# Weight sums of gate and up, and one operand sum, moved from VectorE to GpSimd in a two-FFN decoder layer

## The chip, the cores and the metric

The kernel runs on one core of a Trainium2 chip, in one launch. The metric is the device time of that core in microseconds (us), the median of several executions. PE is TensorE, DVE is VectorE, ACT is ScalarE, POOL is GpSimd and SP is SyncE, whose queue issues nearly all transfers.

## The reference: what is computed

One inference step of a hybrid decoder layer for 1,048 tokens (16 meta tokens, 1,024 prompt tokens, 8 samples), model width 1,024, in float32:

```python
h = h + 0.5 * swiglu(rmsnorm(h, n1), w1g, w1u, w1d)          # first FFN, d_ff = 2816
u = rmsnorm(h, nm) @ w_in                                     # HGRN2 heads and Mamba-2 heads
h = h + concat(hgrn_out, ssm_out) @ w_out
h = h + 0.5 * swiglu(rmsnorm(h, n2), w2g, w2u, w2d)           # second FFN
# swiglu(x, wg, wu, wd) = (silu(x @ wg) * (x @ wu)) @ wd
```

The change touches only the gate and up products `x @ wg` and `x @ wu` of the two FFNs.

## The kernel before

A float32 operand is split into a high part, rounded to the matmul's input format, and a low part, the difference; a product is three matmuls (L163 high by high, L164 high by low, L165 low by high). ACT makes each high part (`hi`, L462 for weights; `cast`, L346 for operands), DVE each low part (`lo`, L466; `low`, L352).

The gate and up products of one block of 128 hidden columns (`pair`) use a Strassen-like scheme: seven block products in place of eight, on sums of weight tiles and sums of operand blocks. `Left` holds the weights of a pair: four loaded tiles of 128x512 in buffers `r` (of which there are eight) and four sums made of them, for products 5, 6, 7 and 3, by `Left.sum_` (L458). A sum is read by `hi` and `lo`, which write the split weight into a buffer `ws`. `Left.plan` says before which product each load, sum, `hi` and `lo` stands. `Blocks` holds the moving operands: `Blocks.sum_` (L341) makes the sums for products 5, 6, 7 and 4, once per half of the tokens and per FFN, on tiles of 128x1048 (first FFN) or 128x1032 (second).

Each FFN has 22 pairs, two to a step `i` of the loop in `ffn`. From `i` = 3 on, the two pairs of a step share part of their work in an inner scheme (`Inner`), with its own small sums and splits on DVE (L586 to L601) and its own evictions (L639 to L646). The text calls these *inner pairs*: eight steps, so eight first and eight second pairs in each FFN. The other six pairs of an FFN are *plain*.

A product accumulates in PSUM. The outer products take turns in two pairs of banks, named `acc`; the inner ones use four single banks, named `mis`. A bank is free for another product when the results have been read out: by ACT (L674), or by DVE at L669, L676, L683, L685, L689, L698 and L703 (`post`), each of which reads one `acc` tile. L643 and L646 read `mis`.

Inside `ffn` the orders of PE, DVE, ACT and SP are written out by hand (`manual_schedule`): each of these engines works through its own list and waits at the head of it. POOL is not in that list, and a scheduler places its instructions. Before the change POOL's work is: constants and masks at the start (L1077 to L1112), the sums of squares for the norms (L230, `tensor_add` on two SBUF tiles), and some memsets.

`first1` and `first2` write out the order at the start of each FFN, where operands are made while the first products run.

Of the kernel before, what the change touches and what calls it, by code (L numbers as in the profile page):

```python
# [316 lines left out]
class Blocks:  # L317
# [19 lines left out]
    def sum_(self, p):  # L337
        x, y = {5: (7, 1), 6: (3, 5), 7: (3, 7), 4: (2, 6)}[p]
        x, y = self.b[x], self.b[y]
        t = self.b[p] if p == 7 else self.new(p)  # L340
        self.K.nc.vector.tensor_sub(t, x, y)  # L341

    def cast(self, p):
        hi = self.K.slot("u", self.K.T, F32R)
# [96 lines left out]
class Left:  # L441
# [12 lines left out]
    def sum_(self, p):  # L454
        x, y, op = {5: (7, 4, ALU.add), 6: (5, 1, ALU.subtract), 7: (1, 7, ALU.subtract), 3: (2, 6, ALU.subtract)}[p]
        if p not in self.raw:
            self.raw[p] = self.K.raw(self.n * P)
        self.K.nc.vector.tensor_tensor(self.raw[p], self.raw[x], self.raw[y], op)  # L458

    def hi(self, p):  # L460
        self.w[p] = self.K.ws()
# [393 lines left out]
def down(K, S, wdv, hidden, src, h, after):  # L855
# [24 lines left out]
    def pieces(p, j, g, b, tag, late=0):  # L880
# [33 lines left out]
        if p in (5, 6, 7, 3):  # L914
            x, y = {5: (21, 22), 6: (0, 11), 7: (22, 0), 3: (12, 0)}[p]
            S.before(b - 9, lambda: sum_(x, y, ALU.add if p == 5 else ALU.subtract))
# [1350 lines left out]
```

## Time and profile before

| | |
|---|---|
| median of 3 runs | 1979.23 us (1977.53 to 1981.9) |
| the profiled execution | 1973.32 us, of which the span is 1971.5 us |
| mean granted TensorE clock | 0.994 |
| PE busy | 1923.6 us (98%) |
| DVE busy | 1529.7 us (78%), 2720 instructions |
| ACT busy | 859.9 us (44%) |
| POOL busy | 82.7 us (4%), 135 instructions |
| gate and up of the first FFN | to about 460 us |
| gate and up of the second FFN | about 1280 to 1700 us |

A row of the timeline has start, duration, engine, line, operation, output<-input tiles, shapes and count, and in brackets the idle time of the engine before it and what ended it. A row of windows has, for a stretch of the span, its length, then the busy time of each engine with its number of instructions, the granted clock, the DMA share and GB/s. The durations of neighbouring DVE rows overlap by some 0.07 us, so the spacing of starts is the time that one takes in a packed queue.

### The profile page before, as it was taken

The numbers are of one execution on the slowest core, as the hardware profiler recorded it, in microseconds if no ns is written. First come the engines' busy times: TensorE is split into PE (matmuls) and PEld (weight loads), VectorE is DVE, ScalarE is ACT, GpSimd is POOL, SyncE is SP. The second block draws the span as 40 slices with busy tenths as digits, with TensorE's granted clock in tenths as the row PEclk, the third lists the DMA queues.
The fourth block names the chain that finished last, engine by engine and source line by source line (L and its number), as shares of the span: only waits on it lengthen the run. The fifth ranks groups of instructions, "written<-read, shape, count | busy, mean of one in ns | idle before, by whom it ended". The sixth has DMA issues, their size and how long they took to land.

```text
span 1971.5 us, 40943 instructions
## 1 busy us (share of the span) xinstructions
PE 1923.6 (98%) x16585; PEld 1885.4 (96%) x16585; DVE 1529.7 (78%) x2720; ACT 859.9 (44%) x1647; POOL 82.7 (4%) x135
## 2 busy tenths in 40 slices
PE   7999999999999999999999999999999999999997
PEld 6999999999999999998988989999999999999997
DVE  7788888888788776675755557888888888878973
ACT  7533232324534555465644535752332333354352
POOL 4000000000001310000000001200000000000000
PEclk9999999999999999999999999999999999999999
DMA  7233333335976632222522153224332333587851
GB/s 220 77 98 97 98 107 96 108 93 171 302 240 214 184 117 61 69 88 73 167 82 72 61 169 126 85 82 119 92 108 87 103 103 112 160 251 230 275 178 68
DMA packets 323877, 258.45 MB, mean 131 GB/s; under 512 B 17568, under 2 KB 299424, under 8 KB 323680
## 3 DMA queue, kind: packets, MB, share of 16 engines
q1 hardware_dynamic: 323448, 255.79, 42.1%
q8 instruction: 131, 2.15, 0.4%
q14 instruction: 58, 0.48, 0.1%
q0 software_dynamic: 224, 0.04, 0.0%
q10 hardware_dynamic: 16, 0.00, 0.0%
HBM read 190.79 MB, written 65.05 MB: 130 GB/s over the span
## 4 chain that ended last, share of the span: by engine, by line
PE 87%; DVE 7%; ACT 2%; DMA 2%; issue 1%; POOL 0%; SPq 0%; DVEq 0%; ACTq 0%; POOLq 0%
PE acc L163 26%; PE acc L165 26%; PE acc L164 26%; PE mis L163 1%; PE mis L165 1%; PE mis L164 1%; DVE u L352 1%; DMA s<-in_x_prompt_dram 1%; PE mis L1725 1%; PE mis L1449 0%; PE mis L1782 0%; DVE ws L466 0%; PE mis L1445 0%; DVE u L341 0%; DVE t L301 0%
## 5 line engine op out<-in xcount | busy, mean ns | idle before, releaser
L163 PE MATMUL acc<-u,ws 128*128 128x258 f32 (+3 forms) x4248 | 1242.9, 293 | 6.7 <-ACT t L674 1.7
L164 PE MATMUL acc<-u,ws 128*128 128x258 f32 (+3 forms) x4248 | 1232.1, 290 | 2.9 <-DVE u L352 2.7
L165 PE MATMUL acc<-u,ws 128*128 128x258 f32 (+3 forms) x4248 | 1231.1, 290 | 3.5 <-DVE ws L466 3.4
L163 PEld LDWEIGHTS acc<-u,ws 128*128 128x128 f32 x4248 | 803.9, 189 | 12.2 <-ACT t L674 2.1
L164 PEld LDWEIGHTS acc<-u,ws 128*128 128x128 f32 x4248 | 806.5, 190 | 5.8 <-DVE u L352 4.0
L165 PEld LDWEIGHTS acc<-u,ws 128*128 128x128 f32 x4248 | 803.6, 189 | 5.2 <-DVE ws L466 4.8
L466 DVE TENSOR_TENSOR ws<-r,ws 128x512 fp32r<-128x512 f32 x276 | 190.6, 691 | 75.0 <-ACT ws L462 74.9
L462 ACT CAST ws<-r 128x512 fp32r<-128x512 f32 x276 | 160.1, 614 | 13.3 <-ACT ws L462 7.8
L458 DVE TENSOR_TENSOR r<-r,r 128x512 f32<-128x512 f32 x176 | 121.5, 692 | 2.7 <-DMA r<-in_w_ffn_up_dram 1.2
L681 ACT ACTIVATE t<-t 128x516 f32<-128x516 f32 (+1 forms) x41 | 26.2, 639 | 212.9 <-DVE t L669 212.9
L712 ACT ACTIVATE t<-t 128x524 f32<-128x524 f32 (+1 forms) x47 | 29.9, 639 | 196.1 <-DVE t L669 196.1
L846 DVE TENSOR_TENSOR u<-u,u 128x1048 fp32r<-128x1048 f32 (+3 forms) x84 | 97.0, 1156 | 5.3 <-ACT u L842 4.5
L669 DVE TENSOR_TENSOR t<-t,u 128x524 f32<-128x524 f32 (+1 forms) x135 | 92.9, 697 | 2.8
L230 POOL TENSOR_TENSOR t<-t,t 128x262 f32<-128x262 f32 (+1 forms) x56 | 54.4, 981 | 823.6 <-ACT t L229 820.4
L158 DVE TENSOR_TENSOR ws<-r,ws 128x512 fp32r<-128x512 f32 x88 | 60.5, 698 | 36.0 <-ACT ws L157 35.6
L903 ACT CAST ws<-u 128x512 fp32r<-128x512 f32 (+1 forms) x72 | 42.2, 586 | 103.2 <-DVE u L898 100.2
L932 DVE SCALAR_TENSOR_TENSOR s<-acc,s 128x524 f32<-128x524 f32 (+3 forms) x88 | 54.6, 643 | 36.9 <-PE acc L165 36.5
L842 ACT CAST u<-u 128x1048 fp32r<-128x1048 f32 (+3 forms) x84 | 82.8, 988 | 0.0
L908 DVE TENSOR_TENSOR ws<-r,ws 128x512 fp32r<-128x512 f32 (+1 forms) x84 | 57.6, 693 | 22.3 <-ACT ws L903 22.2
L903 ACT CAST ws<-r 128x512 fp32r<-128x512 f32 (+1 forms) x84 | 47.9, 582 | 61.6 <-DVE r L898 37.0
L157 ACT CAST ws<-r 128x512 fp32r<-128x512 f32 x88 | 53.7, 618 | 35.6 <-PE acc L165 30.6
L908 DVE TENSOR_TENSOR ws<-u,ws 128x512 fp32r<-128x512 f32 (+1 forms) x72 | 47.4, 658 | 26.8 <-ACT ws L903 26.8
(417 smaller groups left out, 2297.9 us busy)
## 6 DMA issues: line engine op xcount, KB each, us to landing
r<-in_w_ffn_down_dram SPq DMA_DIRECT2D x128, 256.0 KB
hd<-s SPq DMA_DIRECT2D x93, 258.0 KB
r<-in_w_ffn_gate_dram SPq DMA_DIRECT2D x88, 256.0 KB
r<-in_w_ffn_up_dram SPq DMA_DIRECT2D x88, 256.0 KB
hd<-s SPq DMA_DIRECT2D x77, 262.0 KB
u<-hd SPq DMA_DIRECT2D x36, 516.0 KB
u<-hd SPq DMA_DIRECT2D x28, 524.0 KB
r<-in_w_in_dram SPq DMA_DIRECT2D x56, 256.0 KB
```

The lines of the kernel that those rows point to most:

```text
L158: self.nc.vector.tensor_sub(lo, src, hi.bitcast(F32))
L163: mm(ps, whi, xhi, start=first, stop=False, skip_group_check=more)
L164: mm(ps, whi, xlo, start=False, stop=False, skip_group_check=more)
L165: mm(ps, wlo, xhi, start=False, stop=last, skip_group_check=more)
L458: self.K.nc.vector.tensor_tensor(self.raw[p], self.raw[x], self.raw[y], op)
L462: self.K.nc.scalar.copy(self.w[p][:, : self.n * P], self.raw[p])
L466: self.K.nc.vector.tensor_sub(t[:, 512 : 512 + w], self.raw[p], t[:, :w].bitcast(F32))
L669: nc.vector.tensor_mul(t, t if src is None else src, spread.lanes(i, cs))
L842: K.nc.scalar.copy(hi, lo.bitcast(F32))
L846: K.nc.vector.tensor_sub(lo, lo.bitcast(F32), hi.bitcast(F32))
L903: nc.scalar.copy(w[p, j, g][:, : n * P], src)
L908: nc.vector.tensor_sub(t[:, 512 : 512 + n * P], box[0], t[:, : n * P].bitcast(F32))
```

## The change

All 176 weight sums, and 4 of the 16 operand sums (product 7, once for each half of the tokens and each FFN), are issued on POOL in place of DVE.

```diff
@@ class Blocks
         t = self.b[p] if p == 7 else self.new(p)
-        self.K.nc.vector.tensor_sub(t, x, y)
+        eng = self.K.nc.gpsimd if p == 7 else self.K.nc.vector
+        eng.tensor_sub(t, x, y)
@@ class Left
         if p not in self.raw:
             self.raw[p] = self.K.raw(self.n * P)
-        self.K.nc.vector.tensor_tensor(self.raw[p], self.raw[x], self.raw[y], op)
+        self.K.nc.gpsimd.tensor_tensor(self.raw[p], self.raw[x], self.raw[y], op)
```

The changed file has one line more ahead of these places, so its lines are numbered one higher (L458 becomes L459). The orders of PE and SP are the same as before; those of ACT and DVE are the same but for the moved instructions and a few neighbours changing places ahead of the second FFN.

On DVE, in the second pair of an inner step of the first FFN, this stood before (tiles `r` are weights and their sums, `ws` split weights, `acc` products, `s` hidden blocks):

```order
L676 TENSOR_TENSOR t_512_3946<-acc_511_3919,t_509_3912 128x524
L818 TENSOR_TENSOR s_513_3948<-s_474_3633 128x524
L718 TENSOR_TENSOR s_501_3848<-t_488_3741,t_494_3778 128x524
L466 TENSOR_TENSOR ws_514_3950<-r_480_3687,ws_514_3950 128x512
L458 TENSOR_TENSOR r_515_3966<-r_505_3880,r_507_3896 128x512
L458 TENSOR_TENSOR r_516_3968<-r_515_3966,r_504_3878 128x512
L669 TENSOR_TENSOR t_517_3982<-acc_506_3882,u_148_851 128x524
L818 TENSOR_TENSOR s_513_3948<-s_501_3848,s_513_3948 128x524
L458 TENSOR_TENSOR r_505_3880<-r_504_3878,r_505_3880 128x512
L466 TENSOR_TENSOR ws_518_3988<-r_504_3878,ws_518_3988 128x512
```

The same place on DVE has now:

```order
L677 TENSOR_TENSOR t_512_3946<-acc_511_3919,t_509_3912 128x524
L819 TENSOR_TENSOR s_513_3948<-s_474_3633 128x524
L719 TENSOR_TENSOR s_501_3848<-t_488_3741,t_494_3778 128x524
L467 TENSOR_TENSOR ws_514_3950<-r_480_3687,ws_514_3950 128x512
L670 TENSOR_TENSOR t_517_3982<-acc_506_3882,u_148_851 128x524
L819 TENSOR_TENSOR s_513_3948<-s_501_3848,s_513_3948 128x524
L467 TENSOR_TENSOR ws_518_3988<-r_504_3878,ws_518_3988 128x512
```

The sums are gone from between the low part `ws_514` and the read of bank `acc_506`. On POOL the sums of these two inner pairs stand one after the other, with nothing between that would tie them to the place in DVE's list:

```order
L459 TENSOR_TENSOR r_491_3760<-r_480_3687,r_483_3705 128x512
L459 TENSOR_TENSOR r_480_3687<-r_479_3685,r_480_3687 128x512
L459 TENSOR_TENSOR r_492_3762<-r_491_3760,r_479_3685 128x512
L459 TENSOR_TENSOR r_497_3801<-r_484_3707,r_492_3762 128x512
L459 TENSOR_TENSOR r_515_3966<-r_505_3880,r_507_3896 128x512
L459 TENSOR_TENSOR r_505_3880<-r_504_3878,r_505_3880 128x512
L459 TENSOR_TENSOR r_516_3968<-r_515_3966,r_504_3878 128x512
L459 TENSOR_TENSOR r_523_4024<-r_508_3898,r_516_3968 128x512
```

At the start of the first FFN, POOL's list runs from the last masks through the sums of the first pair, the first operand sum, the sums of the second pair and the second operand sum (`u` are operand blocks):

```order
L1082 CAST mask16_8832<-mf_1140_8829 32x16 x4
L459 TENSOR_TENSOR r_53_301<-r_18_147,r_19_149 128x512
L459 TENSOR_TENSOR r_65_346<-r_53_301,r_14_139 128x512
L459 TENSOR_TENSOR r_18_147<-r_14_139,r_18_147 128x512
L459 TENSOR_TENSOR r_71_379<-r_17_145,r_65_346 128x512
L342 TENSOR_TENSOR u_37_223<-u_39_228,u_37_223 128x1048
L459 TENSOR_TENSOR r_121_622<-r_75_394,r_86_444 128x512
L459 TENSOR_TENSOR r_75_394<-r_74_392,r_75_394 128x512
L459 TENSOR_TENSOR r_122_624<-r_121_622,r_74_392 128x512
L459 TENSOR_TENSOR r_126_660<-r_87_446,r_122_624 128x512
L342 TENSOR_TENSOR u_60_323<-u_84_439,u_60_323 128x1048
```

So the first weight sum stands behind the constants, and the second operand sum behind all sums of the second pair.

## The prediction

> **What bounds the kernel now.** I read the page first, then the windows, then the timeline of POOL and DVE side by side.
>
> ```profile
> PE 1923.6 (98%) x16585; PEld 1885.4 (96%) x16585; DVE 1529.7 (78%) x2720; ACT 859.9 (44%) x1647; POOL 82.7 (4%) x135
> L908 DVE TENSOR_TENSOR ws<-r,ws 128x512 fp32r<-128x512 f32 (+1 forms) x84 | 57.6, 693 | 22.3 <-ACT ws L903 22.2
> ```
>
> ```profile
> 35.00:75.00 40.00, 35.00 (x254) 32.90 (x252) 30.23 (x45) 30.73 (x62) 0.00 (x0) 0.96 0.17 54
> 120.00:460.00 340.00, 340.00 (x2791) 339.92 (x2790) 294.32 (x499) 103.46 (x193) 0.00 (x0) 1.00 0.33 101
> 1330.00:1700.00 370.00, 370.00 (x3083) 369.48 (x3082) 319.43 (x542) 113.11 (x211) 0.00 (x0) 1.00 0.34 102
> ```
>
> Through nearly all of gate and up PE is busy in 340.00 of 340 and 370.00 of 370 us: nothing can be gained there by a lighter DVE. Only the starts have idle PE: 5.0 us in 35 to 75, more before it. DVE is not the bound, but at 294 of 340 us it has little room, and it empties PE's banks. POOL has no work at all in these windows, so no row shows POOL beside DVE there. Other places do.
>
> **What a POOL sum costs, and whom.**
>
> ```profile
> L230 POOL TENSOR_TENSOR t<-t,t x56: 730/756/3406, 627.0 to 1287.2; 128x262 f32<-128x262 f32 x28, 128x258 f32<-128x258 f32 x28
> ```
> ```profile
> L1112 POOL TENSOR_TENSOR sel<-sel,s 16x8 f32<-16x8 f32 x1 | 0.2, 193 | 0.0
> ```
> ```profile
> 671.69 2.34 POOL L230 TENSOR_TENSOR t<-t,t 128x262 f32<-128x262 f32 x2 [4.36 <-ACT t L229]
> 1220.81 0.74 POOL L230 TENSOR_TENSOR t<-t,t 128x258 f32<-128x258 f32 x1 [0.26 <-ACT t L229]
> ```
> ```profile
> 671.01 1.24 DVE L846 TENSOR_TENSOR u<-u,u 128x1048 fp32r<-128x1048 f32 x1
> 672.17 2.27 DVE L908 TENSOR_TENSOR ws<-r,ws 128x512 fp32r<-128x512 f32 x2
> 1221.01 0.42 DVE L1850 TENSOR_TENSOR s<-s,acc 128x258 f32<-128x258 f32 x1 [0.80 <-PE acc L165]
> ```
>
> POOL's add takes 0.756 us (median) for 262 columns and 0.193 us for 8: (0.756 - 0.193) / 254 = 2.2 ns a column. My estimate from these is 0.193 + 504 x 2.2 ns = 1.31 us for a weight sum and 2.50 us for 1048 columns. The nearest rows bound a weight sum: not under 0.756, and 0.756 x 512 / 262 = 1.48 if there is no fixed part.
>
> The more important reading is in the pairs of rows. While two POOL adds run from 671.69 to 674.03, the two L908 on DVE take 2.27 us in place of about 1.3 (0.69 each, overlapped), and the adds take 2.34 in place of 1.5. They exclude each other and take turns. L1850, which has one input in PSUM, runs at 1221.01 inside a POOL add and takes its 0.42 us. So a DVE instruction with two SBUF inputs waits out a POOL add whole, and one that reads PSUM goes through, unless it is queued behind one that waits.
>
> The Trainium skill, *SBUF — State Buffer*, section "SBUF: two separate sides", says the same as a rule: GpSimd shares a port pair with VectorE instructions that have two SBUF inputs, as an exclusive lock held for the full instruction; the trace agrees in the 2.27 us above. The skill's *GPSIMD Engine Reference*, section 3.1, gives 4497 ns for a two-input add of 2,048 columns; a quarter of that, an estimate of 1.12 us, would in the layout below leave a stall of 1.2 us in a second inner pair and none in a first, and with smaller starts about 2010 us.
>
> **The change part by part.** *Removed:* 176 sums from DVE. Two in a row take 331.63 to 332.96 (below), 0.65 each: 2.6 us a pair, plus four operand sums of 1.16 us spacing. PE never waits for these in the steady windows, so they buy nothing there by themselves.
>
> *Added:* four POOL sums a pair, 5.2 us in which DVE's two-input work stands still; net 2.6 us of delay in a pair of 20 us. What decides is where they fall. POOL is not tied to DVE's list: a sum starts when its buffers are ready, and the four come in a burst that takes turns with DVE. In the **second inner pair**:
>
> ```profile
> 328.58 0.69 DVE L466 TENSOR_TENSOR ws<-r,ws 128x512 fp32r<-128x512 f32 x1 [0.60 <-ACT ws L462]
> 329.19 0.70 DVE L676 TENSOR_TENSOR t<-acc,t 128x524 f32<-128x524 f32 x1
> 329.80 0.69 DVE L818 TENSOR_TENSOR s<-s 128x524 f32<-128x524 f32 x1
> 330.42 0.70 DVE L718 TENSOR_TENSOR s<-t,t 128x524 f32<-128x524 f32 x1
> 331.03 0.68 DVE L466 TENSOR_TENSOR ws<-r,ws 128x512 fp32r<-128x512 f32 x1
> 331.63 1.41 DVE L458 TENSOR_TENSOR r<-r,r 128x512 f32<-128x512 f32 x2
> 332.96 0.70 DVE L669 TENSOR_TENSOR t<-acc,u 128x524 f32<-128x524 f32 x1
> ```
> ```profile
> 334.00 0.28 PE L163 MATMUL acc<-u,ws 128*128 128x262 f32 x1
> ```
>
> The product that begins at 334.00 writes the bank that L669 reads until 333.66: 0.34 us to spare. The first sum's buffer comes free with the L466 that ends at 329.27 (its last reader), so POOL can begin at 329.3, where DVE had the sum only at 331.63. Taking turns: sum to 330.61, L818 to 331.22, sum to 332.53, L718 to 333.14, sum to 334.45, L466 to 335.06, L669 ends 335.76. PE stalls 1.8 us. With 0.756 us a sum L669 ends at 334.1, a stall of 0.1; with 1.48 us, 2.3.
>
> In the **first inner pair**, POOL's start hangs on the loads. In a plain pair the issue of the up tiles begins at 127.02 and DVE's wait for them ends at 132.83, 5.8 us; here it begins at 306.20, so POOL begins at 312.0:
>
> ```profile
> 127.02 1.14 SPq L452 DMA_DIRECT2D r<-in_w_ffn_up_dram  x2
> ```
> ```profile
> 306.20 1.06 SPq L452 DMA_DIRECT2D r<-in_w_ffn_up_dram  x2
> ```
> ```profile
> 132.83 1.42 DVE L458 TENSOR_TENSOR r<-r,r 128x512 f32<-128x512 f32 x2 [0.55 <-DMA r<-in_w_ffn_up_dram]
> 134.17 0.69 DVE L683 TENSOR_TENSOR t<-acc,t 128x524 f32<-128x524 f32 x1
> ```
> ```profile
> 312.13 0.68 DVE L601 TENSOR_TENSOR ws<-r,ws 128x512 fp32r<-128x512 f32 x1
> 312.73 0.68 DVE L466 TENSOR_TENSOR ws<-r,ws 128x512 fp32r<-128x512 f32 x1
> 313.33 1.41 DVE L458 TENSOR_TENSOR r<-r,r 128x512 f32<-128x512 f32 x2
> 314.66 0.70 DVE L685 TENSOR_TENSOR t<-acc,t 128x524 f32<-128x524 f32 x1
> 316.62 0.42 DVE L601 TENSOR_TENSOR ws<-r,ws 128x256 fp32r<-128x256 f32 x1
> 318.97 0.42 DVE L643 TENSOR_TENSOR t<-mis,t 128x262 f32<-128x262 f32 x1
> ```
> ```profile
> 317.14 0.28 PE L163 MATMUL acc<-u,ws 128*128 128x262 f32 x1
> ```
> ```profile
> 320.83 0.28 PE L163 MATMUL mis<-u,ws 128*128 128x262 f32 x1
> ```
>
> Sum to 313.31, L601 to 313.91, sum to 315.22, L466 to 315.82; L685 goes through beside the third sum and ends at 316.5, ahead of 317.14; L669 waits for that sum until 317.13, the fourth sum ends at 319.04. From L601 to L643 the rows above span 2.35 us, less one removed sum 1.75: L643 starts at 320.79 and ends at 321.2 where PE wants its bank at 320.83. A stall of 0.4 us. If the tiles land 2 us earlier, L685 is 1.2 us late instead; with 0.756 us a sum there is none.
>
> In **plain pairs** (twelve in all) the same layout from 132.8 puts L683, which no longer stands behind two sums, earlier than 134.17. I take 0.
>
> Sixteen inner steps x (1.8 + 0.4) = 35 us; bounds 0 and 16 x (2.3 + 1.2) = 56. When PE has waited, everything later shifts with it, so the relief of 2.6 us has drained the lag by the next burst.
>
> *The starts.*
>
> ```profile
> 17.90 0.68 DVE L458 TENSOR_TENSOR r<-r,r 128x512 f32<-128x512 f32 x1
> ```
> ```profile
> 18.98 0.61 ACT L462 CAST ws<-r 128x512 fp32r<-128x512 f32 x1
> ```
> ```profile
> 19.96 2.62 POOL L1081 CAST mask<-mf 32x16 uint8<-32x16 f32 x4
> ```
> ```profile
> 1280.00:1290.00 10.00, 9.14 (x73) 8.82 (x72) 8.49 (x12) 8.37 (x19) 5.45 (x6) 1.00 0.64 217
> 1290.00:1300.00 10.00, 8.11 (x65) 7.69 (x64) 9.30 (x12) 7.28 (x12) 0.00 (x0) 1.00 0.13 45
> ```
>
> POOL makes constants until 22.58. The first sum, made at 17.90 on DVE, ends at 23.9, and the ACT cast that stood at 18.98 waits for it, with the operand placing and all later casts queued behind: up to 4.9 us. Then seven weight sums and two wide ones, 7 x 1.31 + 2 x 2.50 = 14.2 us, lie beside a DVE that makes PE's low parts, less 4 x 0.65 + 2 x 1.16 = 4.9 of relief: 9.3 us. The first FFN's start costs 0 to 14; I take 8, since part of the holds falls while DVE waits for ACT. The second has 8 x 1.31 + 2 x 2.5 = 15.5 of holds less 7.5 of relief, 8 us, where DVE is busy 8.5 to 9.3 of 10 and PE idles already: 0 to 8, I take 7.
>
> Sum: 35 + 8 + 7 = 50 us. On the profiled execution's own 1973.3 us that is 2023; the median of the runs shown is 5.9 us above it, so the forecast is 1979.2 + 50 = **2029 us**.
>
> **The rivals.**
>
> *DVE and POOL together become the bound.*
>
> ```profile
> 300.00:340.00 40.00, 40.00 (x331) 40.00 (x330) 34.70 (x61) 12.15 (x23) 0.00 (x0) 1.00 0.33 101
> ```
>
> DVE's 34.7 us in 40, less 8 x 0.65, plus 8 x 1.31 of holds is 40.0: full, before any wait. If the 5.3 us of waits stay too, a step takes 45.3: 16 x 5.3 + 15 = 100 us, 2079; with 1.48 us a sum 16 x 6.7 + 22 = 129, 2108. Against it: PSUM readers pass, and waits absorb holds. 0.17.
>
> *Holds fall into DVE's waits; only the starts cost.* Between 0.1 us a step and half a start, 5 to 20 us: 1984 to 1999. It needs sums near 0.8 us. 0.11.
>
> *No change.* The same with free starts, 1979 (1975 to 1983): 0.07.
>
> *Faster.* At the first start PE waits for DVE: 5.0 us idle in 35 to 75. If the 4.9 us taken off DVE there outweigh the holds, that is, if a weight sum holds DVE for under its own 0.65 us, up to 5 us come back: 1974. The Trainium skill, *Perfetto Trace Analysis*, section "Optimizing Scalar/DVE Operations", says that offloading to GPSIMD may make sense when DVE is saturated, and that between these two it might not help, as they share a port; the 2.27 us speak for the second half. 0.04. That the sums stay on DVE is excluded by the order of instructions.
>
> **How the numbers follow.** Forecast (2000 to 2060) 0.61, rivals 0.17, 0.11, 0.07, 0.04. From 1988 (most of the mild case) to 2095 (most of the saturated one) leaves out about 2 in 10. Faster 0.04; within 0.2% (4 us, about what a measurement of this kernel can tell from no change) 0.07; slower 0.61 + 0.17 + 0.11 = 0.89.
>
> **What would show it.** Right: L459 near 1.3 us or more on POOL; DVE's two-input lines with longer means in gate and up, while L683 and L685 keep theirs; PE idle before L163, released by L670 and L644, some 2 us in each 42; windows 120 to 460 no longer at full PE. Wrong: PE still at 340 of 340, or L459 under 0.8 us, or the idle time ended by ACT's `hi` waiting for POOL in the steady pairs, which I take to be early enough.

## The result and the profile after

The changed kernel takes 2006.5 us (2005.07 to 2007.15), the kernel before 1978.38 (1973.2 to 1981.9, four runs each): a ratio of 1.0143, 95% interval 1.0120 to 1.0167, slower by 28 us. The forecast was 2029 us with a range of 1988 to 2095; the direction is that of the forecast and the loss lies where it was put, in the inner steps and at the starts, but the size is 28 us in place of 50.

The page of the changed kernel (busy time of each engine; then groups with busy time and mean ns of one, and the idle time before them with what ended it):

```profile
PE 1941.8 (97%) x16585; PEld 1901.2 (95%) x16585; DVE 1541.3 (77%) x2540; ACT 859.9 (43%) x1647; POOL 356.4 (18%) x315
...
L163 PE MATMUL acc<-u,ws 128*128 128x258 f32 (+3 forms) x4248 | 1248.7, 294 | 22.4 <-DVE t L670 11.6
...
L459 POOL TENSOR_TENSOR r<-r,r 128x512 f32<-128x512 f32 x176 | 262.8, 1501 | 618.4 <-DVE ws L467 253.7
```

DVE lost 180 instructions and is nevertheless busy 11.6 us longer (1541.3 against 1529.7): time in which it stands still behind POOL is recorded as part of its instructions. A weight sum takes 1.50 us on average on POOL. PE waits 11.6 us for L670, a bank read, for which it had no wait on this page before.

The windows of the changed kernel (length, then PE, PEld, DVE, ACT, POOL busy, the granted clock, DMA share, GB/s):

```profile
300.00:340.00 40.00, 39.50 (x324) 39.32 (x323) 35.40 (x52) 11.48 (x22) 12.02 (x8) 1.00 0.31 94
1550.00:1590.00 40.00, 39.12 (x327) 38.94 (x326) 35.23 (x52) 12.04 (x23) 11.01 (x8) 1.00 0.33 100
120.00:460.00 340.00, 336.32 (x2750) 335.24 (x2749) 294.74 (x423) 100.43 (x188) 101.90 (x68) 1.00 0.32 96
```

Where PE was busy for 340.00 of 340 us it is now busy for 336.32. The groups by form of the changed kernel from 220 to 460 us tell which of DVE's instructions grew:

```profile
L819 DVE TENSOR_TENSOR s<-s,s 128x524 f32<-128x524 f32 x18 | 21.2, 1177 | 0.0
L684 DVE TENSOR_TENSOR t<-acc,t 128x524 f32<-128x524 f32 x12 | 8.4, 700 | 0.4
```

and the same groups of the kernel before:

```profile
L818 DVE TENSOR_TENSOR s<-s,s 128x524 f32<-128x524 f32 x18 | 12.5, 695 | 0.0
L683 DVE TENSOR_TENSOR t<-acc,t 128x524 f32<-128x524 f32 x12 | 8.4, 700 | 0.4
```

Same size, same window: with both inputs in SBUF 0.695 became 1.177 us, with one in PSUM 0.700 stayed 0.700.

**Where the 28 us went.** PE runs the same 16585 matmuls in the same order in both kernels, so the start of the same matmul in two profiled executions can be subtracted. The table gives by how much each kernel falls behind in each stretch (stretches are times of the kernel before; worked out from the starts of PE's instructions in the traces; us). "Middle" is code that no variant touches: it moves by 0 to 8 us from one execution to another, and the two largest, 6.7 and 8.1, are in the longest execution of e2 and of e7. Each row is one execution. The first column also holds up to 1.5 us from the arrival of the first loads, ahead of 20 us, and one jump of 0.65 us at 91 us of the kernel before, in the kernels that have the whole sums of the fourth pair on POOL (the changed kernel, e1, e3, e5). From 20 to 60 us e4 loses 5.5 us and the changed kernel 8.5, though both have the same sums on POOL there: so much can one execution differ from another at a start.

| kernel | first start, to 110 | plain, 110 to 200 | inner, 200 to 460 | middle, 460 to 1240 | second start, to 1420 | inner, 1420 to 1720 |
|---|---|---|---|---|---|---|
| changed kernel | 8.8 | -0.2 | 5.9 | 3.9 | 5.6 | 8.1 |
| e1_weights | 6.4 | -0.2 | 6.1 | 0.5 | 4.5 | 8.2 |
| e2_operands | 4.4 | 0.1 | 0.0 | 6.7 | 4.8 | 0.2 |
| e3_not_starts | 0.4 | -0.2 | 6.3 | 4.0 | -0.4 | 7.5 |
| e4_starts | 6.0 | -0.2 | 0.0 | 1.1 | 5.7 | 0.1 |
| e5_plain | 1.4 | -0.2 | 0.0 | 3.8 | -0.4 | 0.1 |
| e6_second | 2.2 | -0.2 | 2.6 | 0.5 | -0.4 | 3.4 |
| e7_first | 3.0 | 0.1 | 3.3 | 8.1 | -0.4 | 4.1 |
| e8_half | 5.8 | -0.2 | 6.4 | 1.5 | 3.7 | 7.7 |
| e9_extra_adds | 17.7 | 19.3 | 54 | 1 | 32.8 | 59.5 |
| e10_extra_memset | -0.1 | -0.2 | 0.0 | -0.1 | 5.9 | 0.1 |
| e11_odd63 | 0.9 | -0.2 | 0.0 | 0.4 | -0.2 | -0.9 |
| e12_first_63 | 0.3 | -0.1 | 0.2 | 3.8 | -0.4 | 0.9 |

Without the middle the changed kernel loses 8.8 - 0.2 + 5.9 + 5.6 + 8.1 = 28.2 us, the 28.1 of the medians: 14.4 at the two starts (0.65 of it the jump at 91 us), 14.0 in the inner steps, nothing in the plain pairs after them. With starts that vary so much, the close agreement of 28.2 and 28.1 is partly chance.

### The profile page after: what moved, and what is told of

It reads as the page before. It is cut to its first block, busy times and chain, and to the rows that moved or that the text cites. A ratio compares the mean times of both kernels' runs of the same rounds, so it can differ in the third digit from the quotient of the medians.

```text
span 2005.2 us, 41209 instructions
## 1 busy us (share of the span) xinstructions
PE 1941.8 (97%) x16585; PEld 1901.2 (95%) x16585; DVE 1541.3 (77%) x2540; ACT 859.9 (43%) x1647; POOL 356.4 (18%) x315
## 4 chain that ended last, share of the span: by engine, by line
PE 74%; DVE 17%; issue 4%; ACT 3%; POOL 1%; DMA 1%; DVEq 0%; SPq 0%; POOLq 0%; ACTq 0%
PE acc L163 22%; PE acc L165 22%; PE acc L164 22%; DVE ws L467 2%; DVE t L670 2%; DVE s L719 1%; DVE ws L602 1%; DVE u L353 1%; DVE s L819 1%; ACT ws L463 1%; PE mis L1726 1%; DVE t L647 1%; DVE t L677 1%; DVE u L847 1%; PE mis L163 1%
## 5 line engine op out<-in xcount | busy, mean ns | idle before, releaser
L163 PE MATMUL acc<-u,ws 128*128 128x258 f32 (+3 forms) x4248 | 1248.7, 294 | 22.4 <-DVE t L670 11.6
L459 POOL TENSOR_TENSOR r<-r,r 128x512 f32<-128x512 f32 x176 | 262.8, 1501 | 618.4 <-DVE ws L467 253.7
L467 DVE TENSOR_TENSOR ws<-r,ws 128x512 fp32r<-128x512 f32 x276 | 224.7, 815 | 76.7 <-ACT ws L463 76.7
L463 ACT CAST ws<-r 128x512 fp32r<-128x512 f32 x276 | 160.0, 616 | 14.6 <-PE mis L165 7.3
L230 POOL TENSOR_TENSOR t<-t,t 128x262 f32<-128x262 f32 (+1 forms) x56 | 54.0, 975 | 359.9 <-ACT t L229 356.6
L670 DVE TENSOR_TENSOR t<-t,u 128x524 f32<-128x524 f32 (+1 forms) x135 | 98.4, 738 | 2.8
L158 DVE TENSOR_TENSOR ws<-r,ws 128x512 fp32r<-128x512 f32 x88 | 61.6, 711 | 36.1 <-ACT ws L157 35.7
L719 DVE TENSOR_TENSOR s<-t,t 128x524 f32<-128x524 f32 (+1 forms) x88 | 75.7, 870 | 1.5
```

What stands on the lines that cost most here:

```text
L163: mm(ps, whi, xhi, start=first, stop=False, skip_group_check=more)
L459: self.K.nc.gpsimd.tensor_tensor(self.raw[p], self.raw[x], self.raw[y], op)
L463: self.K.nc.scalar.copy(self.w[p][:, : self.n * P], self.raw[p])
L467: self.K.nc.vector.tensor_sub(t[:, 512 : 512 + w], self.raw[p], t[:, :w].bitcast(F32))
L670: nc.vector.tensor_mul(t, t if src is None else src, spread.lanes(i, cs))
L719: nc.vector.tensor_mul(halves(hid[0][:, n * 2 * K.Q : n * 2 * K.Q + 2 * K.Q])[:, cs], temp(f"g{n}", cs), temp(f"u{n}", cs))
```

## The experiments

Lines in the variants are up to four higher than in the kernel before: L669 is L670 in the changed kernel and in e1, L673 in e9 and e10, L672 in the others.

**The weight sums alone (e1), the operand sums alone (e2).**

```diff
# e1_weights, from the changed kernel, Blocks.sum_
-        eng = self.K.nc.gpsimd if p == 7 else self.K.nc.vector
+        eng = self.K.nc.vector
# e2_operands, from the changed kernel, Left.sum_; where the pair's Left is made: left.pool = lambda p: False
-        self.K.nc.gpsimd.tensor_tensor(self.raw[p], self.raw[x], self.raw[y], op)
+        eng = self.K.nc.gpsimd if self.pool(p) else self.K.nc.vector
+        eng.tensor_tensor(self.raw[p], self.raw[x], self.raw[y], op)
```

> The four operand sums are back on VectorE, the 176 weight sums stay on GpSimd. Theory (holds: a GpSimd add stops VectorE's two-input work for its whole length, and PE pays where that pushes a bank read or a low part past the time PE wants it): the inner pairs cost what they cost in the changed kernel (5.9 us in the first FFN, 7.9 in the second, by PE's progress in the profiles), the starts lose four wide holds, from 8.8 + 5.7 to about 10 together; total 24 us over before. Rival (late results: ACT's casts wait for sums that GpSimd makes later and slower): the second operand sum no longer stands behind the second pair's sums, so the starts fall to about 5 and the total to 19.

> Only the four operand sums on GpSimd, all weight sums on VectorE. Theory (holds): nothing in the inner pairs; at the starts four holds of 2.5 us less 1.2 of relief each, of which PE sees a part: 2 to 5 us in all. Rival (late results): the casts of product 7 wait 1.3 us more each, but the first is no longer behind the constants' sums: 0 to 3 us.

Measured: e1 1999.86 us, ratio 1.0111 (1.0091 to 1.0131); e2 1982.97, 1.0029 (1.0016 to 1.0041). In the inner steps e1 loses what the whole change loses and e2 nothing: the loss there is of the weight sums alone. At the starts e1 loses 6.4 + 4.5 us, about the 10 of its theory and not the 5 of the rival. The four operand sums by themselves cost 5.1 us by the medians. The 4.4 and 4.8 us of e2's row are more than that, but they are from the longest of its ten executions (1989.79 us), and 1.4 of the 4.4 came with the first loads. By the medians the two parts nearly add up: 22.0 + 5.1 = 27.1 of 28.1 us.

**The starts alone (e4), all but the starts (e3).** `f` counts the pairs of an FFN from 0.

```diff
# from the changed kernel, Left.sum_; left.pool is set where the pair's Left is made
-        self.K.nc.gpsimd.tensor_tensor(self.raw[p], self.raw[x], self.raw[y], op)
+        eng = self.K.nc.gpsimd if self.pool(p) else self.K.nc.vector
+        eng.tensor_tensor(self.raw[p], self.raw[x], self.raw[y], op)
# e3_not_starts: left.pool = lambda p: f > 1   (operand sums on vector)
# e4_starts:     left.pool = lambda p: f < 2   (operand sums as changed)
```

> The weight sums of the first two pairs of each FFN and the operand sums are back on VectorE; the other twenty pairs of each FFN keep their sums on GpSimd. Theory (holds): both starts as before, inner pairs as in the changed kernel: 14 us over before. Rival (VectorE and GpSimd together are the bound): the inner pairs cost the same 14. Rival (the starts' lag carries on into the pairs): under 8.

> Only the weight sums of the first two pairs of each FFN and the four operand sums on GpSimd. Theory (holds, and the first sums behind the constants): the starts cost 8.8 + 5.7 = 14.5 us and nothing follows. If the lag of a start carries on into the later pairs: more than 18.

Measured: e3 1992.22 us, 1.0074 (1.0054 to 1.0094), that is 14.6 us; e4 1990.5, 1.0065 (1.0043 to 1.0087), 12.9 us. Together 27.5 of 28: starts and inner steps are two separate losses of nearly equal size.

**One kind of pair at a time (e5, e6, e7).** The same edit with the operand sums on vector.

```diff
# e5_plain:  left.pool = lambda p: 2 <= f < 6
# e6_second: left.pool = lambda p: f >= 6 and f % 2 == 1
# e7_first:  left.pool = lambda p: f >= 6 and f % 2 == 0
```

> Sums on GpSimd only in the plain pairs after the first two (four pairs in each FFN), all else as before. Theory (holds): holds there fall into VectorE's waits and ahead of bank reads with time to spare: within 2 us of before, as PE's progress in the changed kernel showed (8.8 us late at 110 and 8.6 at 200). Rival (net load of VectorE is what counts): 8 pairs at 2.6 us of net hold, up to 10 us.

> Sums on GpSimd only in the second inner pair of each step (eight pairs in each FFN), all else as before. Theory (holds): in the changed kernel two holds fall ahead of the read L669 of a bank that had 0.35 us to spare, so nearly all of the inner cost is here: 12 us over before, PE's waits ended by that line. Rival (VectorE and GpSimd together are the bound): half of the burst load, under 4 us.

> Sums on GpSimd only in the first inner pair of each step, all else as before. Theory (holds): the holds push L685 and L643 back, but both still end before PE wants the bank in the changed kernel: 0 to 2 us over before. Rival (VectorE and GpSimd together are the bound): the same as with the second pairs alone.

Measured: e5 1977.65 us, 0.9996 (0.9982 to 1.0010); e6 1981.79, 1.0029 (1.0019 to 1.0039); e7 1985.45, 1.0047 (1.0030 to 1.0065). Plain pairs cost nothing that the medians show; PE's starts show the one jump of 0.65 us at 91 us. The second pairs cost 6.0 us by PE's starts, half of the 12 expected, and the first 7.4, where 0 to 2 were expected. By its size alone, 7.4 beside 6.0 is what the rival of e7 foretold (VectorE and GpSimd together the bound, so both kinds of pair cost the same); what speaks against it is where PE waits, and e11 and e12 below. What PE waits for in e7, from 220 to 480 us and from 1440 to 1720 us (us in total, times, longest):

```profile
PE acc L163 <- DVE t L672: 1.0, 3, 0.4
```
```profile
PE acc L163 <- DVE t L672: 3.3, 7, 0.6
```

It is the same read as in e6, in the *second* pair, where e7 has no sum on POOL. All seven jumps of PE against the kernel before from 200 to 460 us stand at that one matmul of a step, and seven more in the second FFN; only three of the first seven are long enough to be listed as waits above. There are seven and not eight, in e6 and in the changed kernel too: the sums of the first inner step of an FFN are made while the last plain pairs run (from 154.90 us in e7), and no jump follows them. How the first pair's lateness gets there, e7's timeline shows, POOL first, then ACT, then DVE:

```profile
315.34 6.84 POOL L460 TENSOR_TENSOR r<-r,r 128x512 f32<-128x512 f32 x4 [33.83 <-DVE r L595]
```
```profile
329.71 0.64 ACT L715 ACTIVATE t<-t 128x524 f32<-128x524 f32 x1 [8.03 <-DVE t L672]
330.26 0.60 ACT L464 CAST ws<-r 128x512 fp32r<-128x512 f32 x1
```
```profile
328.99 0.69 DVE L672 TENSOR_TENSOR t<-t,u 128x524 f32<-128x524 f32 x1
330.90 0.69 DVE L468 TENSOR_TENSOR ws<-r,ws 128x512 fp32r<-128x512 f32 x1 [1.22 <-ACT ws L464]
337.80 0.70 DVE L672 TENSOR_TENSOR t<-acc,u 128x524 f32<-128x524 f32 x1
```

In the kernel before the ACT row stood here:

```profile
324.87 0.64 ACT L712 ACTIVATE t<-t 128x524 f32<-128x524 f32 x1 [7.59 <-DVE t L669]
```

POOL's burst is over at 322.18, and DVE sits idle for 1.22 us ahead of 330.90, yet it makes up nothing. It waits there for a cast (`hi`) that stands in ACT's list behind L715; L715 waits for DVE's L672 of 328.99. L715 is 4.84 us later than before, and so are the cast, DVE's low part (330.90 against 326.06) and the bank read (337.80 against 332.96), while PE was then 4.39 us later: 0.45 us of lateness carried through an idle time of 1.22 us. A wait absorbs lateness only if what it waits for does not itself wait for the late engine.

**Half of every sum (e8).**

```diff
# from the changed kernel, Left.sum_ (operand sums as changed)
-        self.K.nc.gpsimd.tensor_tensor(self.raw[p], self.raw[x], self.raw[y], op)
+        n = self.n * P // 2
+        for eng, cs in ((self.K.nc.gpsimd, slice(0, n)), (self.K.nc.vector, slice(n, 2 * n))):
+            eng.tensor_tensor(self.raw[p][:, cs], self.raw[x][:, cs], self.raw[y][:, cs], op)
```

> Every weight sum is split by columns: 256 on GpSimd, 256 on VectorE; the operand sums as in the changed kernel. Theory (holds): a GpSimd add of 256 columns holds 0.75 us in place of 1.31, and VectorE's half stands again in its list; in a second inner pair two holds of 0.75 and two halves of 0.35 come to about what the two whole sums took: 0 to 0.5 us a step, 0 to 8 in all; starts still 8 to 12; total about 14 over before. Rival (late results): the starts as in the changed kernel, 14.5, as the first sum still waits for the constants, and inner pairs 0.

Measured: 2001.8 us, 1.0127 (1.0110 to 1.0144), and in the inner steps 14.1 us, as much as with whole sums and more than the 0 to 8 expected. The timeline of e8, second pair, POOL and then DVE:

```profile
338.23 1.90 POOL L461 TENSOR_TENSOR r<-r,r 128x256 f32<-128x256 f32 x2 [14.37 <-DVE ws L469]
341.37 0.85 POOL L461 TENSOR_TENSOR r<-r,r 128x256 f32<-128x256 f32 x1 [1.24 <-DVE ws L469]
```
```profile
338.68 0.85 DVE L821 TENSOR_TENSOR s<-s 128x524 f32<-128x524 f32 x1
339.45 1.24 DVE L721 TENSOR_TENSOR s<-t,t 128x524 f32<-128x524 f32 x1
341.21 1.29 DVE L461 TENSOR_TENSOR r<-r,r 128x256 f32<-128x256 f32 x2
343.65 0.41 DVE L461 TENSOR_TENSOR r<-r,r 128x256 f32<-128x256 f32 x1
```

Two half sums hold L821 and L721 for 0.16 and 0.54 us (against 0.69 and 0.70), less than the whole ones do. But DVE's own two halves ahead of the read take 1.29 us, where two whole sums took 1.33, so nothing is given back: one half alone takes 0.41 us (343.65), and these two lie beside POOL's third half sum (341.37), a third hold ahead of the read. The size of a hold alone does not tell its cost; the relief and the number of holds have to be set against it.

**POOL's reads without relief (e9), POOL's writes alone (e10).** Both from the kernel before; what they add goes to a tile of 100 columns that nobody reads.

```diff
# e9_extra_adds, ahead of each weight sum on DVE
+        for i in range(4):
+            cs = slice(100 * i, 100 * i + 100)
+            self.K.nc.gpsimd.tensor_tensor(self.K.extra, self.raw[x][:, cs], self.raw[y][:, cs], op)
# e10_extra_memset, ahead of each weight sum on DVE
+        self.K.nc.gpsimd.tensor_copy(self.K.extra[:, :1], self.raw[x][:, :1])
+        for i in range(12):
+            self.K.nc.gpsimd.memset(self.K.extra, 0.0)
```

> The kernel before, with all its sums on VectorE, and beside each weight sum four GpSimd adds of 100 columns of the same two tiles into a scratch tile that nothing reads. Theory (holds): VectorE is held without any relief, some 0.4 us sixteen times a pair, 6.5 us in 20: more than the changed kernel, 40 to 120 us over before, with PE's waits ended by VectorE's bank reads. Rival (late results): nobody waits for these adds, so 0, or a few us where they delay the freeing of a weight buffer.

> The kernel before, and beside each weight sum one GpSimd copy of a single column and twelve memsets of 100 columns of a scratch tile that nothing reads: GpSimd is about as busy as in the changed kernel, but reads next to nothing. Theory (holds by reading: the Trainium skill, SBUF - State Buffer, says that a VectorE instruction with two SBUF inputs contends only with a GpSimd one that reads SBUF): 0 to 4 us over before. If any work of GpSimd holds VectorE: as with the extra adds, over 20 us.

Measured: e9 2157.28 us, 1.0905 (1.0884 to 1.0927), 179 us, more than the 40 to 120 expected; e10 1983.0, 1.0021 (1.0009 to 1.0034), 4 us. e9 does not price what it was meant to. DVE's waits in e9:

```profile
DVE r L462 <- POOL extra L461: 130.3, 44, 4.5
```

One sum of each of the 44 pairs overwrites a tile that POOL still reads, and DVE waits for that, 130.3 us in all. The 179 us are such a wait, of the program's own, and holds together, and the time of e9 does not tell them apart. From 220 to 460 us the wait is 26.8 us, while the mean of the line with both inputs in SBUF (L822 here) grew only from 0.695 to 0.738 us.

e10 does answer its question. Its window:

```profile
300.00:340.00 40.00, 40.00 (x331) 40.00 (x330) 34.72 (x61) 12.11 (x24) 20.82 (x104) 1.00 0.33 101
```

and its group, from 220 to 460 us, of the line that went from 0.695 to 1.177 us in the changed kernel:

```profile
L822 DVE TENSOR_TENSOR s<-s,s 128x524 f32<-128x524 f32 x18 | 12.5, 696 | 0.0
```

POOL is busy for 20.82 us of 40 with writing, more than the 12.02 of the changed kernel, and DVE's 34.7 us and the 0.696 us of L822 are what they were without it. So DVE is not held by POOL's being busy or writing, but by adds that read SBUF. This agrees with the Trainium skill, *SBUF — State Buffer*, section "SBUF: two separate sides", which limits the lock against a VectorE instruction with two SBUF inputs to a GpSimd op that reads SBUF.

The 5.9 us of e10 lie at the second start, and their cause is another, POOL's queue. PE's waits in e10 and in the changed kernel, 1240 to 1440 us:

```profile
PE mis L255 <- POOL t L231: 6.2, 1, 6.2
```
```profile
PE mis L254 <- POOL t L230: 1.2, 1, 1.2
```

L230 is the norm's sum of squares, which POOL makes for the second FFN's operands; the memsets stood in front of it. In the changed kernel three weight sums start at 1282.48 in front of one, and cost 1.2 us in the same place.

**Only the sums behind the critical read (e11).** Products 6 and 3 of the second inner pairs:

```diff
# e11_odd63 (operand sums on vector): left.pool = lambda p: f >= 6 and f % 2 == 1 and p in (6, 3)
```

> As the run with sums on GpSimd only in the second inner pairs, but only those of products 6 and 3; 5 and 7 are on VectorE again. Theory (holds): no hold falls ahead of L669 any more, as the sum for product 6 needs the sum for product 5, which stands just ahead of L669: 0 us over before (within 2). Rival (VectorE and GpSimd together are the bound): half of what four sums cost.

Measured: 1974.69 us, 0.9990 (0.9979 to 1.0001); 32 sums on POOL, none in front of the read at L672, and PE does not wait for L672 in the steady windows. The interval reaches 1: a gain is not shown. In its profile the seven steps of the second FFN are 0.13 us shorter each (the -0.9 of the table): there the read was a little late in the kernel before already, so a sum less ahead of it did give something back.

**The lateness of the first pair, and one sum less in front of the read (e12).** This tells whether the 7.4 us of e7 arise in the second pair, as read above, or in the first.

```diff
# e12_first_63 (operand sums on vector): left.pool = lambda p: f >= 6 and (f % 2 == 0 or p in (6, 3))
```

> All four weight sums of the first inner pairs go to POOL, and of the second inner pairs only the sums for products 6 and 3, of which one stood on DVE ahead of the bank read at L672 (L669 of the kernel before). Theory: the lateness that the first pair's holds leave on DVE (0.45 us in the first FFN, 0.52 in the second) is carried round ACT's list into the second pair, where it first meets a read with nothing to spare, 0.20 us in the first FFN and none in the second; one sum less ahead of that read takes 0.6 us off it, so it is on time in both FFNs, no PE wait for L672 remains in the steady windows, and the inner pairs cost 0 to 1 us in place of the 7 us of the first pairs alone: ratio 0.999 to 1.001. Rival: the holds of the first pairs cost PE where they lie, at the reads of the first pair: then the 7 us stay, ratio 1.003 to 1.005. Second rival: the sums of products 6 and 3 slip ahead of the read and hold it too: 10 us or more, ratio 1.005 or above.

Measured: 1979.41 us, 1.0011 (1.0001 to 1.0022). The inner steps cost 0.2 and 0.9 us in place of e7's 3.3 and 4.1, with 32 sums more on POOL. The timeline of e12, POOL and then DVE, and a window:

```profile
311.47 6.49 POOL L460 TENSOR_TENSOR r<-r,r 128x512 f32<-128x512 f32 x4 [14.10 <-DMA r<-in_w_ffn_up_dram]
333.07 1.29 POOL L460 TENSOR_TENSOR r<-r,r 128x512 f32<-128x512 f32 x1 [15.11 <-DVE r L460]
```
```profile
332.85 0.70 DVE L672 TENSOR_TENSOR t<-acc,u 128x524 f32<-128x524 f32 x1
333.46 1.46 DVE L821 TENSOR_TENSOR s<-s,s 128x524 f32<-128x524 f32 x1
```
```profile
300.00:340.00 40.00, 40.00 (x331) 40.00 (x330) 35.31 (x55) 12.31 (x23) 8.91 (x6) 1.00 0.32 99
```

The burst in the first pair is there (6.49 us, 6.84 in e7), and PE is full again: 40.00 of 40. The read begins at 332.85, 0.11 us earlier than the 332.96 of the kernel before, and the hold (1.46 in place of 0.69) falls behind it. The ratio is at the upper edge of the 0.999 to 1.001 of the theory; both rivals of this run wanted 1.003 or above. So 96 of the 176 sums can go to POOL at a cost of some 2 us; none of the variants is shown to be faster than the kernel before.

## Why the prediction came out as it did

**The mechanism held.** POOL's sum takes 1.26 us at least and 1.50 on average (estimate 1.31, bounds 0.756 to 1.48 without waiting; the lower estimate of 1.12 is under even the shortest sum). Instructions with two SBUF inputs wait, PSUM readers pass (1.177 and 0.700 us above). PE's idle time in the steady windows is ended by the bank read L670; relief of DVE bought nothing that the medians show (0.9996 in e5; at most the 0.13 us a step of e11's second FFN).

**Plain pairs: 0 predicted; one jump of 0.65 us found at 91 us, with the sums of the fourth pair, and -0.2 us from 110 to 200.**

**The inner steps: 16 x 2.2 = 35 us predicted, 14.0 found. This is the term that was mis-sized.** The loss is made of fourteen jumps of PE, not sixteen, as the first inner step of each FFN costs nothing: seven of 0.73 to 1.29 us in the first FFN (5.9) and seven of 0.99 to 1.31 in the second (8.0). Both halves of the 2.2 were laid out wrongly. For the second pair the prediction put three sums ahead of the read, taking turns with L818, L718 and L466. POOL and then DVE in the changed kernel:

```profile
341.13 3.00 POOL L459 TENSOR_TENSOR r<-r,r 128x512 f32<-128x512 f32 x2 [12.02 <-DVE ws L467]
345.37 1.28 POOL L459 TENSOR_TENSOR r<-r,r 128x512 f32<-128x512 f32 x1 [1.24 <-DVE ws L467]
```
```profile
340.36 0.69 DVE L467 TENSOR_TENSOR ws<-r,ws 128x512 fp32r<-128x512 f32 x1 [0.61 <-ACT ws L463]
340.97 0.70 DVE L677 TENSOR_TENSOR t<-acc,t 128x524 f32<-128x524 f32 x1
341.58 1.41 DVE L819 TENSOR_TENSOR s<-s 128x524 f32<-128x524 f32 x1
342.91 1.78 DVE L719 TENSOR_TENSOR s<-t,t 128x524 f32<-128x524 f32 x1
344.62 0.68 DVE L467 TENSOR_TENSOR ws<-r,ws 128x512 fp32r<-128x512 f32 x1
345.22 0.69 DVE L670 TENSOR_TENSOR t<-acc,u 128x524 f32<-128x524 f32 x1
```
```profile
346.05 0.36 PE L163 MATMUL acc<-u,ws 128*128 128x262 f32 x1 [0.49 <-DVE t L670]
```

Two sums fall ahead of it, not three: the third waits until 345.37 for the low part of 344.62, which still reads the buffer that it overwrites. The prediction had checked the first sum's buffer and not the third's. Two holds lengthen L819 by 0.72 and L719 by 1.08 us (against 0.69 and 0.70), 1.80 together, and the two sums taken out of DVE's list there gave back 1.33: 0.47 us net.

For the first pair the prediction let L643 miss its bank by 0.4 us; PE does not wait there. POOL and then DVE there, in the changed kernel:

```profile
322.44 6.68 POOL L459 TENSOR_TENSOR r<-r,r 128x512 f32<-128x512 f32 x4 [14.16 <-DMA r<-in_w_ffn_up_dram]
```
```profile
322.91 0.70 DVE L684 TENSOR_TENSOR t<-acc,t 128x524 f32<-128x524 f32 x1
323.53 1.02 DVE L602 TENSOR_TENSOR ws<-r,ws 128x512 fp32r<-128x512 f32 x1
324.47 1.78 DVE L467 TENSOR_TENSOR ws<-r,ws 128x512 fp32r<-128x512 f32 x1
...
326.89 1.07 DVE L670 TENSOR_TENSOR t<-t,u 128x524 f32<-128x524 f32 x1
327.88 1.51 DVE L602 TENSOR_TENSOR ws<-r,ws 128x256 fp32r<-128x256 f32 x1
```

Before, the last four took 0.68, 0.68, 0.70 and 0.42 us: the burst holds DVE for 2.90 us. The prediction's own layout comes to more: it began the burst at 312.0 us and held the first of these four for 1.18 us (313.31 for 312.13). The burst began 0.96 us earlier in the step (322.44 less PE's 11.40 us of lateness there is 311.04), so most of its first sum lies beside L684, which reads PSUM and takes its 0.70 us, and the hold of L602 is 0.34 us. Against some 2.5 given back the burst leaves DVE 0.38 us late, and e7 and e12 show that this is paid at the second pair's read. At 340.36 of the rows above DVE is 11.78 us later than before (328.58), PE 11.40. The sum is then 0.38 + 0.47 = 0.85 us of lateness against a spare of 0.20 (the prediction's 0.34, less the 0.14 that lie between the end of the read and the start of the matmul, 345.91 to 346.05): 0.65 us, and PE's matmul goes from 334.00 to 346.05, 12.05 later, 0.65 more than the 11.40 ahead of it. Each half alone would give 0.47 - 0.20 = 0.27 and 0.45 - 0.20 = 0.25, and e6 and e7 show jumps of 0.28 and 0.25 us at this matmul. (The next matmul adds 0.08 us in each, which makes the changed kernel's jump 0.73 us here.) In the second FFN there is no spare: at the same place of its timeline DVE is 0.52 us late from the first pair, with 0.47 from the second that is 0.99 us, and PE's jump is 1.00.

So the prediction's sentence that the relief drains the lag by the next burst was wrong: lateness survives DVE's two waits, since they wait for ACT and ACT for DVE. This error and the layout of the third sum had opposite signs.

**The starts: 8 + 7 = 15 us predicted, 8.8 + 5.6 = 14.4 found.** POOL, then ACT in the changed kernel's first start:

```profile
21.68 5.55 POOL L459 TENSOR_TENSOR r<-r,r 128x512 f32<-128x512 f32 x4
27.18 3.40 POOL L342 TENSOR_TENSOR u<-u,u 128x1048 f32<-128x1048 f32 x1
```
```profile
22.97 0.62 ACT L463 CAST ws<-r 128x512 fp32r<-128x512 f32 x1 [4.27 <-POOL r L459]
```

The first sum stood behind the constants, until 21.68 (22.58 expected), and the cast of 18.98 came 3.99 us later (up to 4.9 expected). The agreement of the sums at the starts is luck in good part. The prediction did not price the norm's adds queued behind sums at the second start (1.2 us), nor the clock below. Its 9.3 us for the first start set the relief of four weight sums against the holds of seven; seven would make it 7.3. And from 20 to 60 us e4 lost 5.5 us where the changed kernel lost 8.5. How much of the two starts is holds and how much late results was not measured apart.

**The rivals.** DVE and POOL as the bound: excluded, PE is still busy 97%, and DVE's windows are at 35.4 of 40 us, stalls included. Only the starts cost: half true, e4 is that kernel, at 12.9 us. No change and faster: excluded by the interval.

## What to carry to other kernels

When work moves from VectorE to GpSimd, price each instruction by its net hold on the VectorE chain (time that VectorE's two-SBUF-input instructions grow, less the time taken off VectorE ahead of the same deadline), and find the next read that has nothing to spare: here about 0.4 to 0.5 us a pair against a spare of 0 to 0.20 us made all of the steady loss. A moved instruction that falls behind that read costs nothing, so which ones to move is settled by every buffer and queue that sets their start, not by their number. And count a wait as a cushion only after following what it waits for: if that goes back to the late engine, the lateness passes through.

## What the runs showed of the hardware that was not expected

The granted clock was lower where the first start was delayed. Windows of the kernel before, then of the changed one:

```profile
20.00:30.00 10.00, 7.60 (x57) 6.41 (x56) 9.12 (x12) 9.09 (x22) 2.45 (x4) 1.00 0.94 245
30.00:40.00 10.00, 6.99 (x51) 6.10 (x50) 7.85 (x11) 9.76 (x26) 0.00 (x0) 1.00 0.46 157
```
```profile
20.00:30.00 10.00, 6.18 (x29) 4.97 (x28) 5.25 (x4) 4.94 (x12) 9.57 (x11) 0.67 0.95 229
30.00:40.00 10.00, 8.80 (x43) 8.03 (x43) 4.91 (x9) 7.07 (x16) 4.42 (x4) 0.52 0.39 126
```

From 20 to 40 us the clock was 1.00 before and 0.67 and then 0.52 after, and PE, busy for 8.80 of 10 us, got through 43 matmuls where 51 had taken 6.99. e1 and e4, whose first start is delayed too, show 0.83 and 0.66 there, e3, whose start is not, 1.00 and 1.00. Dips are not tied to sums on POOL, though: the kernel before shows 0.83 from 40 to 50 us, and e7, whose start has no sum on POOL but whose first loads came 1.5 us later, 0.83 and 0.83 from 20 to 40. The delayed starts went with slower matmuls besides their waits; how much of the 8.8 us that is, and which caused which, was not measured apart. The Trainium skill, *TensorE: Matmul & The Clock Gate*, section "Part 1: The HAM clock gate", says that a gate sets PE's clock by how busy PE has been of late. A stalled start would fit that, but windows of 10 us do not show the rule: PE busy for 6.99 of 10 kept 1.00 before, and 8.80 of 10 had 0.52 after.

POOL and DVE share by turns: POOL's median sum is 1.61 us against 1.26 at the least, so POOL too stands waiting, and a burst of four in a first inner pair lasts 6.2 to 6.8 us, not the 5.0 of four shortest sums.
